# New order of the recurrence's steps, of the first head's projections and of two broadcasts in the mixer layers of a two-block transformer kernel

## The chip, the cores and the metric

One core of one Trainium2 chip runs the whole kernel in one launch. The metric is the device time of one execution in microseconds (us). The engines are TensorE (PE in the profile, with its weight loads as PEld), VectorE (DVE), ScalarE (ACT), GpSimd (POOL) and SyncE (SP, which issues most DMAs). Each takes its own queue of instructions in the order in which the program has put them there, and waits where an instruction needs the result of another engine.

## The reference

The model has two blocks, each of two layers, on one sequence of 512 tokens with 1024 features, all in fp32. The change touches only the mixer of the second block's layers, which the reference writes so:

```python
xn = rms_norm_2(h, attn_norm_g[layer])
u_ssm, u_g, v_g, q, k, v = jnp.split(xn @ w_in[layer], [o1, o2, o3, o4, o5], axis=-1)
y_ssm  = s5_mixer(u_ssm, ...)              # linear recurrence over the tokens, GELU, gated linear unit
y_sgu  = spatial_gating(u_g, v_g, ...)     # tokens mixed in windows of 128
y_diff = diff_attention(q, k, v, ...)      # 4 heads, each softmax(c=0) - lambda * softmax(c=1)
h = h + jnp.concatenate([y_ssm, y_sgu, y_diff], axis=-1) @ w_out[layer]
```

The recurrence takes 256 channels, the gating 256 and the attention 512 (four heads of 128, with two queries and two keys of 64 each). Both y_diff and q and k are normalised row by row.

## The kernel before

A matrix product in fp32 is made of three matmuls in a faster format (mm3, L133 to L135): weights and activations are each split into a high and a low part, on ACT (L95, L97) and on DVE or POOL (L107 to L111). A projection (proj in second_layer) is 24 such matmuls into one bank of PSUM. token_major makes values with tokens on the partitions, in 96 smaller matmuls (L1685 to L1687) for half of the columns.

The code emits instructions for all engines in one stream, and a scheduler with a simulated timeline orders each engine's queue by priority, which is the place in the code; late(n) moves what it encloses back by n places. So the order of the code sets the order of the queues, except where the scheduler sees something ready earlier.

PSUM is divided by tags: `BANKS = dict(mm=2, sc=2, tp=2, o=1, st=1)`. Tag o has one bank. It holds po, the output of a head (L1768), and also, by TG["bk"], the key broadcast that keys makes (L192, from the tile that L187 fills); the table's names for it are pso in both cases. Tag st (psst) holds the output broadcast bo, the rotation's matmuls (L1703) and the row factors of L657. Tag mm (psmm) holds projections and every third group of scores, sc (pssc) other scores and token_major, tp (pstp) the transposed tiles (L279), the statistics (L1713), the gating (L1612, L1613) and the recurrence.

One mixer layer runs so. Two projections make u for the recurrence (L1671). main then makes the gating's values (token_major) and two projections for its other half (L1798), the gating itself (gmlp, L1592 to L1619: L1606 on DVE makes its normalised operand, L1612 and L1613 multiply, L1616 multiplies the result), V in two halves, then the projections, rotation and statistics of head 0 and head 1 (prepare), the key broadcasts (keys) and the attention of four heads (attend), into which the projections of heads 2 and 3 (nx) and, from head 3 on, parts of the output projection (out_part) are woven. s5 is a generator with three steps behind its loads: the matmuls and scans of the recurrence (L1494 to L1513), the matmuls of its output and the write to memory that reorders it (L1523 to L1540), and GELU and gated linear unit (L1543 to L1569). main counts work in `done`, and where it passes an entry of S5_AT the next step of s5 is emitted.

attend walks four tiles of queries: scores (L1750, mask L1751), maximum (L1754, L1756, L1757), exponential (L1760), the difference of the two softmaxes (L1763 to L1765), transposed to pT (L279, L281), product with V into po (L1768). At a head's end ACT reads po twice (L1771, L1772), token_factor makes the row norm (L657 to L664), and L187, L192 and L1782 multiply it in. keys turns the statistics of prepare (L1716 to L1722) into a broadcast (L187, L192) and multiplies the keys (L1732).

The layer runs twice, as mixer 0 from about 1640 to 1905 us and as mixer 1 from about 2262 to 2528 us of the span.

Of the kernel before, what the change touches and what calls it, by code (L numbers as in the profile page):

```python
# [1622 lines left out]
def second_layer(s, L):  # L1623
    nc, a, mixp = s.nc, s.a, s.mixp
# [49 lines left out]
    def token_major(w):  # L1674

        pv = [s.P(TG["tok"]), s.P(TG["tok"])]
        ps = [pv[c // 2][:, (c % 2) * 256:(c % 2) * 256 + 256] for c in range(NT)]
        for g in range(2):
            wh, wl = s.load(w[:, g * 1024:g * 1024 + 1024])
            for k4 in range(4):  # L1680
                k = 4 * g + k4
                for c in range(NT):
                    q = slice(c * 128, c * 128 + 128)
                    w0, w1 = wh[:, k4 * 256:k4 * 256 + 256], wl[:, k4 * 256:k4 * 256 + 256]
                    nc.tensor.matmul(ps[c], s.xh[k][:, q], w0, start=k == 0 and c % 2 == 0, stop=False)  # L1685
                    nc.tensor.matmul(ps[c], s.xh[k][:, q], w1, start=False, stop=False)
                    nc.tensor.matmul(ps[c], s.xl[k][:, q], w0, start=False, stop=k == KT - 1 and c % 2 == 1)  # L1687
        return ps
# [3 lines left out]
    def prepare(h):  # L1692
        sqs, qk = [], []
        for which in range(2):
            ps = proj(4 + 2 * h + which)
            sq, raw, t2 = s.T(), s.T(), s.T()
            t1 = s.A((128, S), F32)
            nc.scalar.activation(raw, ps, AF.Copy)
            nc.scalar.activation(sq, raw, AF.Square)
            nc.vector.scalar_tensor_tensor(t1, raw, gq[:, 2 * which:2 * which + 1], tabs[0], ALU.mult, ALU.mult)  # L1700
            p2 = s.P(TG["perm"])
            with s.late(L_PERM):
                nc.tensor.matmul(p2, perm, raw, start=True, stop=True)  # L1703
            nc.vector.scalar_tensor_tensor(t2, p2, gq[:, 2 * which + 1:2 * which + 2], tabs[1], ALU.mult, ALU.mult)
            nc.gpsimd.tensor_add(t1, t1, t2)
            sqs.append(sq)
            qk.append(t1)
            yield 6
        N = (128, 2, NT, 2)
        ps = s.P(TG["stat"])  # L1710
        for x in range(2):
            for c in range(NT):
                nc.tensor.matmul(ps[:, 8 * x + 2 * c:8 * x + 2 * c + 2], sqs[x][:, c * 128:(c + 1) * 128], s.headind, start=True, stop=True)  # L1713
        v = s.small(N, tag="hfv")
        rb, rb2 = (x.unsqueeze(1).unsqueeze(3).to_broadcast(list(N)) for x in (s.rt, s.rt2))
        nc.vector.tensor_mul(v, ps[:, 0:16].rearrange("p (x c t) -> p x c t", x=2, t=2), rb2)  # L1716

        nc.vector.tensor_scalar(v[:, 0], v[:, 0], 1.0, 64 * EPS, ALU.mult, ALU.add)
        nc.vector.tensor_scalar(v[:, 1], v[:, 1], 1.0 / 64, EPS, ALU.mult, ALU.add)
        y = s.rsqrt(v.rearrange("p x c t -> p (x c t)"), (128, 16))  # L1720
        f = s.small(N, tag="hff", bufs=4)
        nc.vector.tensor_mul(f, y.rearrange("p (x c t) -> p x c t", x=2, t=2), rb)  # L1722
        heads[h] = (f, qk[0], qk[1])
        yield 1

    def keys(h):
        f, Q, Kt = heads[h]
        with s.late(L_KEYS):
            bk = s.bcast_rows(f[:, 1], 2, eng="a", tag=TG["bk"])
        for c in range(2):  # L1730
            r = slice(64 * c, 64 * c + 64)
            nc.vector.tensor_mul(KP[h % 2][c][r], bk[r], Kt[r])  # L1732

    def attend(h):
        f, Q, Kt = heads[h]
        K = KP[h % 2]
        po = s.P("o")
        lsum = s.small((128, 2, NT), tag="dls")
        for i in range(NT):
            n = i + 1  # L1740
            w = n * 128
            q = slice(i * 128, i * 128 + 128)
            m, sc, pp = s.small((128, 2), tag="dm", bufs=6), [], []
            if n <= 2:
                ps = s.P(SCB[(NT * h + i) % len(SCB)])
            for c in range(2):
                if n > 2:
                    ps = s.P(SCB[(NT * h + i) % len(SCB)])
                o = c * w if n <= 2 else 0
                nc.tensor.matmul(ps[:, o:o + w], Q[:, q], K[c][:, :w], start=o == 0, stop=False)  # L1750
                nc.tensor.matmul(ps[:, o + w - 128:o + w], s.identr, s.chunked, start=False, stop=n > 2 or c == 1)  # L1751
                sc.append(ps[:, o:o + w])
                if n > 2:
                    nc.vector.tensor_reduce(m[:, c:c + 1], sc[c], AX.X, ALU.max, negate=True)  # L1754
            if n <= 2:
                nc.vector.tensor_reduce(m, ps[:, :2 * w].rearrange("p (c k) -> p c k", c=2), AX.X, ALU.max, negate=True)  # L1756
            nc.vector.tensor_mul(m, m, f[:, 0, i])  # L1757
            for c in range(2):
                p = s.sp.tile([128, 512], F32, name="p", tag="p")
                nc.scalar.activation(p[:, :w], sc[c], AF.Exp, bias=m[:, c:c + 1], scale=f[:, 0, i, c:c + 1], accum_out=lsum[:, c, i:i + 1])  # L1760
                pp.append(p)
            r = s.small((128, 1), tag="dr", bufs=6)
            nc.vector.reciprocal(r, lsum[:, 1, i:i + 1])  # L1763
            nc.vector.tensor_scalar(r, r, lsum[:, 0, i:i + 1], nlam, ALU.mult, ALU.mult)
            nc.vector.scalar_tensor_tensor(pp[0][:, :w], pp[1][:, :w], r, pp[0][:, :w], ALU.mult, ALU.add)  # L1765
            pT = transposed(s, pp[0], n)
            for j in range(n):
                nc.tensor.matmul(po[:, q], V[j][:, h * 128:h * 128 + 128], pT[:, j * 128:j * 128 + 128], start=j == 0, stop=j == n - 1)  # L1768
            yield 0.6 * n
        ot, sq = s.T(), s.T()  # L1770
        nc.scalar.activation(sq, po, AF.Square)  # L1771
        nc.scalar.activation(ot, po, AF.Copy)  # L1772
        r0 = s.small((128, NT), tag="dr0")
        nc.vector.reciprocal(r0, lsum[:, 0])
        f = token_factor(s, [sq], inds[:, 0], 128, r0, li)
        if h == 3:
            live.append(out_part(s, w_out, *LAST, range(1, KT, 2)))
            for g in live:
                for w in g:
                    pass  # L1780
        bo = s.bcast_rows(f.unsqueeze(2), 1, eng="a")
        nc.vector.tensor_mul(ot, bo, ot)  # L1782
        s.dbg("d_diff%d_%d" % (L, h), ot)
        mix_tile(s, 4 + h, ot, gq[:, 4:5])
        yield 1
# [5 lines left out]
    def main():  # L1791
        ug = []
        vps = token_major(a["w_in_2_vg"][L])
        yield 10
        for x in range(2):
            ps = proj(2 + x)
            t = s.A((128, 512), F32)
            nc.vector.tensor_mul(t, ps, s.rb)  # L1798
            ug.append(t)
            yield 5  # L1800
        yield from gmlp(s, L, gtabs, vps, ug)
        for x in range(2):
            ps = token_major(a["w_in_2_v"][L, x])
            for c in range(NT):
                if x == 0:
                    V[c] = s.A((128, 512), F32)
                nc.scalar.activation(V[c][:, 256 * x:256 * x + 256], ps[c], AF.Copy, scale=s.rt[:, c:c + 1])
            yield 10
        yield from prepare(0)
        keys(0)  # L1810
        yield from prepare(1)
        for h in range(4):
            if h < 3:
                keys(h + 1)
            nx = prepare(h + 2) if h < 2 else iter(())
            if h in PARTS:
                while len(live):
                    next(live[0], None) is None and live.pop(0)
                live.append(out_part(s, w_out, *PARTS[h]))
            for w in attend(h):  # L1820
                x = 0.0
                while live and x < w * PART_RATIO:
                    c = next(live[0], None)
                    if c is None:
                        live.pop(0)
                    else:
                        x += c
                yield w + next(nx, 0)
            for w in nx:
                yield w  # L1830
# [3 lines left out]
    next(side)  # L1834
    done, at, n = 0.0, S5_AT, 0
    for w in main():
        done += w
        while n < len(at) and done >= at[n]:
            next(side, None)
            n += 1  # L1840
# [4 lines left out]
TG = dict(s5b=("tp", "tp"), s5y=("tp", "tp"), perm="st", gm="tp", bk="o", stat="tp", tok="sc")  # L1845
L_PERM = 0
L_KEYS = 40
S5_AT = [12, 34, 60]
SCB = ["sc", "sc", "mm"]
PARTS = {3: (0, 4)}  # L1850
LAST = (4, 6)
# [310 lines left out]
```

## Time and profile before

| | us |
|---|---|
| timed runs, median of 3 (lowest to highest) | 2903.78 (2902.26 to 2911.31) |
| profiled execution | 2889.64 |
| its span | 2887.9 |
| TensorE busy in it | 2756.0 |
| mean granted clock of TensorE | 0.972 of full speed |

The span runs from the first to the last instruction; the profiled execution's own time has 1.7 us more around it. The profile gives each engine's busy time, what ended its idle time (the releaser), and the TensorE clock that was granted, as a share of full speed. Times in the rows are microseconds from the start of the span.

### The profile page before, as it was taken

What the parts mean: (1) busy time and instruction counts of PE and PEld (TensorE: products, weight loads), DVE (VectorE), ACT (ScalarE), POOL (GpSimd) and SP (SyncE); (2) the same over time, 40 slices, a digit from 0 to 9 for tenths busy, and PEclk for the clock granted to TensorE, in tenths of its full rate; (3) what the DMA queues carried; (4) which work ended last, traced back from release to release, by engine and by line L of the source; (5) the groups of instructions that cost most, each with busy time, mean ns of one, the idle gap of its engine ahead of it and who ended that gap; (6) DMA issues with size and microseconds to landing.
All of it is one profiled execution on the core that took longest, in us unless ns stands there. A gap on an engine that the chain in (4) does not pass through costs nothing.

```text
span 2887.9 us, 41501 instructions
## 1 busy us (share of the span) xinstructions
PE 2756.0 (95%) x15403; PEld 2344.7 (81%) x15403; DVE 1745.4 (60%) x3366; ACT 1271.7 (44%) x2305; POOL 820.8 (28%) x668
## 2 busy tenths in 40 slices
PE   7989999999999899999999789999999898999999
PEld 6766678888888799999999777778888776788887
DVE  3667669465454567666666536776375536775473
ACT  3555553223322466666666414444243224443342
POOL 3310024232112154555555221032023211122120
PEclk8979999999999899999999899999999999999999
DMA  3200123334332276776777732132333320232322
GB/s 129 94 27 22 34 79 131 95 130 140 105 95 66 75 249 203 247 225 225 242 225 249 217 109 67 34 109 87 106 97 103 124 70 15 76 95 89 108 89 94
DMA packets 123192, 344.67 MB, mean 119 GB/s; under 512 B 16610, under 2 KB 28162, under 8 KB 122468
## 3 DMA queue, kind: packets, MB, share of 16 engines
q1 hardware_dynamic: 111968, 320.60, 35.3%
q0 software_dynamic: 5680, 17.19, 1.8%
q10 hardware_dynamic: 5332, 4.14, 0.5%
q8 instruction: 123, 2.02, 0.3%
q14 instruction: 89, 0.73, 0.1%
HBM read 326.39 MB, written 15.48 MB: 118 GB/s over the span
## 4 chain that ended last, share of the span: by engine, by line
PE 55%; DVE 4%; POOL 3%; ACT 2%; issue 2%; DMA 1%; SPq 0%; another core or an unknown queue 0%; POOLq 0%; DVEq 0%; ACTq 0%
PE psmm L1050 5%; PE psmm L133 5%; PE psmm L134 5%; PE psmm L135 5%; PE pssc L1050 5%; PE pstp L133 3%; PE pstp L135 3%; PE pstp L134 3%; PE pssc L133 3%; PE pssc L135 3%; PE pssc L134 3%; PE psmm L1051 2%; PE pssc L1051 2%; POOL wlo L109 1%; DVE wlo L111 1%
## 5 line engine op out<-in xcount | busy, mean ns | idle before, releaser
L95 ACT ACTIVATE whi<-raw 128x1024 fp32r<-128x1024 f32 (+5 forms) x687 | 629.1, 918 | 900.7 <-PE psmm L134 326.9
L111 DVE TENSOR_TENSOR wlo<-raw,whi 128x1024 fp32r<-128x1024 f32 (+4 forms) x605 | 728.8, 1208 | 381.1 <-ACT whi L95 345.5
L1050 PE MATMUL psmm<-A,whi 128*128 128x320 f32 x1120 | 302.9, 348 | 3.4 <-DVE T L1056 1.8
L133 PE MATMUL psmm<-xh,whi 128*128 128x512 f32 x688 | 277.7, 405 | 11.6 <-ACT xh L97 8.3
L134 PE MATMUL psmm<-xl,whi 128*128 128x512 f32 x688 | 274.2, 399 | 3.9 <-DVE xl L107 3.9
L1050 PE MATMUL pssc<-A,whi 128*128 128x320 f32 x992 | 272.7, 351 | 2.3 <-ACT whi L95 1.4
L135 PE MATMUL psmm<-xh,wlo 128*128 128x512 f32 x688 | 273.8, 398 | 0.1
L1051 PE MATMUL psmm<-A,wlo 128*128 128x160 f32 x1120 | 265.5, 239 | 0.0
L1051 PE MATMUL pssc<-A,wlo 128*128 128x160 f32 x992 | 238.6, 242 | 5.2 <-DVE wlo L111 4.8
L109 POOL TENSOR_TENSOR wlo<-raw,whi 128x1024 fp32r<-128x1024 f32 (+2 forms) x82 | 196.3, 2397 | 163.6 <-ACT whi L95 138.6
L109 POOL TENSOR_TENSOR A<-T,A 128x160 fp32r<-128x160 f32 (+2 forms) x166 | 184.0, 1110 | 123.7 <-ACT A L95 123.5
L1050 PEld LDWEIGHTS psmm<-A,whi 128*128 128x128 f32 x1120 | 210.2, 188 | 7.0 <-DVE T L1056 5.3
L1051 PEld LDWEIGHTS psmm<-A,wlo 128*128 128x128 f32 x1120 | 213.6, 191 | 0.6
L1051 PEld LDWEIGHTS pssc<-A,wlo 128*128 128x128 f32 x992 | 191.1, 193 | 9.4 <-DVE wlo L111 7.2
L1050 PEld LDWEIGHTS pssc<-A,whi 128*128 128x128 f32 x992 | 187.7, 190 | 4.5 <-ACT whi L95 2.7
L1876 POOL TENSOR_TENSOR T<-T 128x512 f32<-128x512 f32 x44 | 57.1, 1297 | 415.8 <-DVE T L1873 358.7
L135 PE MATMUL pssc<-xh,wlo 128*128 128x512 f32 x448 | 175.2, 391 | 0.0
L134 PE MATMUL pssc<-xl,whi 128*128 128x512 f32 x448 | 175.2, 391 | 0.0
L133 PE MATMUL pssc<-xh,whi 128*128 128x512 f32 x448 | 174.9, 390 | 0.0
L95 ACT ACTIVATE A<-T 128x160 fp32r<-128x160 f32 (+2 forms) x178 | 85.8, 482 | 185.2 <-POOL T L1072 97.4
L133 PEld LDWEIGHTS psmm<-xh,whi 128*128 128x128 f32 x688 | 132.2, 193 | 41.0 <-ACT xh L97 8.3
L134 PEld LDWEIGHTS psmm<-xl,whi 128*128 128x128 f32 x688 | 132.1, 192 | 35.0 <-DVE xl L107 6.8
(614 smaller groups left out, 6137.3 us busy)
## 6 DMA issues: line engine op xcount, KB each, us to landing
raw<-moe_gu SPq DMA_DIRECT2D x176, 512.0 KB, 4.5
raw<-w_up_t SPq DMA_DIRECT2D x88, 512.0 KB, 3.5
raw<-moe_dn SPq DMA_DIRECT2D x64, 384.0 KB, 3.5
raw<-ffn_gu SPq DMA_DIRECT2D x44, 512.0 KB, 3.7
raw<-moe_dn SPq DMA_DIRECT2D x64, 320.0 KB, 3.3
raw<-od_w_in_t SPq DMA_DIRECT2D x24, 512.0 KB, 3.5
raw<-w_in_t SPq DMA_DIRECT2D x24, 512.0 KB, 3.5
raw<-w_down_t SPq DMA_DIRECT2D x32, 384.0 KB, 3.0
```

The source lines that it names most:

```text
L95: nc.scalar.activation(out, x, AF.Copy)
L109: nc.gpsimd.tensor_sub(out, x, h.bitcast(F32))
L111: nc.vector.tensor_sub(out, x, h.bitcast(F32))
L133: nc.tensor.matmul(ps, wh, xh, start=first, stop=False)
L134: nc.tensor.matmul(ps, wh, xl, start=False, stop=False)
L135: nc.tensor.matmul(ps, wl, xh, start=False, stop=last)
L1050: nc.tensor.matmul(ps[:, :2 * CAP], wh, x, start=first, stop=False)
L1051: nc.tensor.matmul(ps[:, :CAP], wl, x[:, :CAP], start=False, stop=last)
L1876: nc.gpsimd.tensor_mul(acc[1], acc[1], acc[0])
```

## The change

It adds and removes no instruction; it moves some. S5_AT goes from [12, 34, 60] to [26, 48, 72], so that the three steps of the recurrence are emitted later: the first behind the gating, the second behind prepare(0), the third behind prepare(1). prepare(0) is emitted ahead of the second half of V. keys(h+1) is emitted behind the first tile of attend(h) and no more ahead of attend(h). The output broadcast bo of the first three heads is put back by L_OUT = 40 places. The new code's lines behind L1781 are one to three higher.

```diff
--- before.py
+++ after.py
@@ -1778,7 +1778,8 @@
             for g in live:
                 for w in g:
                     pass
-        bo = s.bcast_rows(f.unsqueeze(2), 1, eng="a")
+        with s.late(L_OUT if h < 3 else 0):
+            bo = s.bcast_rows(f.unsqueeze(2), 1, eng="a")
         nc.vector.tensor_mul(ot, bo, ot)
         s.dbg("d_diff%d_%d" % (L, h), ot)
         mix_tile(s, 4 + h, ot, gq[:, 4:5])
@@ -1800,24 +1801,25 @@
             yield 5
         yield from gmlp(s, L, gtabs, vps, ug)
         for x in range(2):
+            if x == 1:
+                yield from prepare(0)
             ps = token_major(a["w_in_2_v"][L, x])
             for c in range(NT):
                 if x == 0:
                     V[c] = s.A((128, 512), F32)
                 nc.scalar.activation(V[c][:, 256 * x:256 * x + 256], ps[c], AF.Copy, scale=s.rt[:, c:c + 1])
             yield 10
-        yield from prepare(0)
         keys(0)
         yield from prepare(1)
         for h in range(4):
-            if h < 3:
-                keys(h + 1)
             nx = prepare(h + 2) if h < 2 else iter(())
             if h in PARTS:
                 while len(live):
                     next(live[0], None) is None and live.pop(0)
                 live.append(out_part(s, w_out, *PARTS[h]))
-            for w in attend(h):
+            for i, w in enumerate(attend(h)):
+                if i == 1 and h < 3:
+                    keys(h + 1)
                 x = 0.0
                 while live and x < w * PART_RATIO:
                     c = next(live[0], None)
@@ -1845,7 +1847,8 @@
 TG = dict(s5b=("tp", "tp"), s5y=("tp", "tp"), perm="st", gm="tp", bk="o", stat="tp", tok="sc")
 L_PERM = 0
 L_KEYS = 40
-S5_AT = [12, 34, 60]
+S5_AT = [26, 48, 72]
+L_OUT = 40
 SCB = ["sc", "sc", "mm"]
 PARTS = {3: (0, 4)}
 LAST = (4, 6)
```

The queue of DVE around the gating of mixer 0, before. psmm is a projection, pssc the gating's values, pstp a product of the recurrence or of the gating.

```order
L1798 TENSOR_TENSOR A_19180<-psmm_19155,rb_18896 128x512 [waits PE_49]
...
L111 TENSOR_TENSOR wlo_19529<-raw_19526,whi_19528 128x1024 [waits DMAHW6_49,PE_49,Activation_49]
L1502 TENSOR_TENSOR A_19219<-pstp_19182,s5E_19008 128x512 [waits DMAHW4_49,PE_49]
...
L1511 TENSOR_TENSOR A_19231<-A_19219,s5E_19008 128x512 [waits DVE_49]
L1507 SCALAR_TENSOR_TENSOR A_19224<-A_19216,A_19224 128x512 [waits Pool_49]
L1511 TENSOR_TENSOR A_19236<-A_19224,s5E_19008 128x512 [waits DVE_49]
L1798 TENSOR_TENSOR A_19272<-psmm_19247,rb_18896 128x512
L1606 SCALAR_TENSOR_TENSOR A_19297<-pssc_19039,rsy4_19283,vgain_18900 128x256
...
L1616 TENSOR_TENSOR A_19180<-pstp_19305,A_19180 64x512 [waits PE_49]
```

The same place of DVE now:

```order
L1799 TENSOR_TENSOR A_19180<-psmm_19155,rb_18896 128x512 [waits PE_49]
...
L1799 TENSOR_TENSOR A_19213<-psmm_19188,rb_18896 128x512 [waits PE_49]
L1606 SCALAR_TENSOR_TENSOR A_19238<-pssc_19039,rsy4_19224,vgain_18900 128x256 [waits DVE_49]
...
L111 TENSOR_TENSOR wlo_19462<-raw_19459,whi_19461 128x1024 [waits DMAHW6_49,Activation_49]
L1616 TENSOR_TENSOR A_19180<-pstp_19246,A_19180 64x512 [waits PE_49]
...
L111 TENSOR_TENSOR wlo_19504<-raw_19501,whi_19503 128x1024 [waits DMAHW7_49,Activation_49]
L1502 TENSOR_TENSOR A_19319<-pstp_19282,s5E_19008 128x512 [waits DMAHW4_49,PE_49]
...
L1511 TENSOR_TENSOR A_19331<-A_19319,s5E_19008 128x512 [waits DVE_49]
...
L1511 TENSOR_TENSOR A_19336<-A_19324,s5E_19008 128x512 [waits DVE_49]
```

The four L1606 and the L1616 now stand ahead of the recurrence's L1502 to L1511, and not behind them.

The queue of TensorE at the end of head 0 of mixer 0, before. pso_19920 is po of head 0, pso_20178 the key broadcast of head 2, psst_20140 the row factor and psst_20166 the output broadcast of head 0; A_18927 is the keys of head 2.

```order
L1768 MATMUL pso_19920<-pT_20128,A_19457 128x128
L133 MATMUL psmm_20279<-xh_18727,whi_20275 128x512 [waits PE_49,Activation_49]
...
L657 MATMUL psst_20140<-pack_all_81,T_20135 128x2 [waits Activation_49]
...
L1750 MATMUL pssc_20375<-A_18930,A_19833 128x512 [waits PE_49,Activation_49]
...
L192 MATMUL psst_20166<-pack_all_81,T_20164 128x128 [waits Activation_49]
...
L192 MATMUL pso_20178<-pack_all_81,T_20176 128x128 [waits Activation_49]
...
L1750 MATMUL psmm_20453<-A_18927,A_19977 128x128 [waits DVE_49]
```

The same place now; here pso_19911 is po of head 0, pso_20001 the key broadcast of head 1, A_18929 and A_18930 are the keys of head 1, and psmm_20279 is a projection of head 3.

```order
L1768 MATMUL pso_19911<-pT_20128,A_19457 128x128
L657 MATMUL psst_20140<-pack_all_81,T_20135 128x2 [waits Activation_49]
...
L192 MATMUL pso_20001<-pack_all_81,T_19999 128x128 [waits PE_49,Activation_49]
...
L1750 MATMUL pssc_20179<-A_18929,A_19793 128x128 [waits DVE_49]
...
L1750 MATMUL pssc_20179<-A_18930,A_19793 128x128 [waits DVE_49]
...
L192 MATMUL psst_20166<-pack_all_81,T_20164 128x128 [waits PE_49,Activation_49]
...
L133 MATMUL psmm_20279<-xh_18727,whi_20275 128x512 [waits Activation_49]
```

Before, the broadcast in bank o behind head 0 was that of head 2, and scores of head 1 stood ahead of it; now it is that of head 1, and all scores of head 1 stand behind it.

## Rows read from the trace of the kernel before

**Rows 1.** The page: busy time of each engine, and engines on the chain that ended last.
```profile
PE 2756.0 (95%) x15403; PEld 2344.7 (81%) x15403; DVE 1745.4 (60%) x3366; ACT 1271.7 (44%) x2305; POOL 820.8 (28%) x668
...
PE 55%; DVE 4%; POOL 3%; ACT 2%; issue 2%; DMA 1%; SPq 0%; another core or an unknown queue 0%; POOLq 0%; DVEq 0%; ACTq 0%
```

**Rows 2.** TensorE's waits, mixer 0 (1630 to 1910 us): total us, times, longest.
```profile
PE pstp L1612 <- DVE A L1606: 8.7, 1, 8.7
...
PE pso L192 <- ACT T L187: 3.9, 1, 3.9
PE psmm L133 <- ACT p L1760: 3.7, 2, 2.0
PE psst L192 <- ACT T L187: 2.9, 1, 2.9
...
PE pso L1768 <- ACT pT L281: 0.7, 1, 0.7
```

**Rows 3.** TensorE's waits, mixer 1 (2255 to 2530 us), lines that differ.
```profile
PE psmm L133 <- ACT p L1760: 3.9, 2, 2.2
PE pso L192 <- ACT T L187: 3.8, 1, 3.8
...
PE pssc L1750 <- ACT p L1760: 0.8, 1, 0.8
```

**Rows 4.** Windows: span of each, busy us (instructions) by engine, granted clock, DMA.
```profile
1680.80:1691.00 10.20, 4.79 (x21) 4.49 (x22) 6.37 (x9) 0.00 (x0) 6.05 (x5) 0.50 0.01 2
1694.30:1697.80 3.50, 3.50 (x17) 3.41 (x17) 0.68 (x1) 0.00 (x0) 0.00 (x0) 0.52 0.00 0
1700.00:1720.00 20.00, 20.00 (x193) 18.63 (x193) 3.82 (x4) 4.66 (x8) 1.15 (x3) 1.00 0.16 54
1730.00:1735.00 5.00, 5.00 (x24) 4.14 (x23) 1.89 (x2) 1.56 (x3) 0.00 (x0) 1.00 1.05 379
1759.30:1766.10 6.80, 4.22 (x10) 2.89 (x11) 5.07 (x14) 2.86 (x5) 0.53 (x1) 0.50 0.00 1
1813.90:1817.30 3.40, 3.10 (x10) 2.21 (x11) 2.91 (x5) 3.07 (x7) 0.00 (x0) 0.50 0.00 0
1830.60:1838.00 7.40, 5.39 (x27) 4.40 (x27) 5.22 (x22) 4.57 (x12) 0.00 (x0) 1.00 0.00 1
1840.00:1860.00 20.00, 20.00 (x113) 16.58 (x112) 15.16 (x47) 11.77 (x29) 0.00 (x0) 1.00 0.09 27
2452.20:2459.00 6.80, 4.90 (x12) 3.85 (x13) 3.68 (x21) 3.75 (x11) 0.00 (x0) 0.50 0.00 0
```

**Rows 5.** Timeline around the gating, mixer 0: start, us, instruction, [idle before <-releaser].
```profile
1675.29 1.06 ACT L95 ACTIVATE whi<-raw 128x1024 fp32r<-128x1024 f32 x1 [4.38 <-PE psmm L134]
...
1675.41 2.09 PE L1494 MATMUL pstp<-s5U,A 128*64 128x64 f32 x64
...
1684.38 0.69 DVE L1511 TENSOR_TENSOR A<-A,s5E 128x512 f32<-128x512 f32 x1
...
1685.59 1.65 DVE L1606 SCALAR_TENSOR_TENSOR A<-pssc,rsy,vgain 128x256 f32<-128x256 f32 x4
...
1687.38 2.50 POOL L1513 TENSOR_TENSOR A<-A 128x512 f32<-128x512 f32 x2
```

**Rows 6.** Timeline between head 0's statistics and the first key broadcast, mixer 0.
```profile
1758.36 0.23 DVE L1716 TENSOR_TENSOR hfv<-pstp,rt 128x16 f32<-128x16 f32 x1
...
1761.20 0.63 ACT L187 ACTIVATE T<-hff 128x512 f32<-128x512 f32 x1 [4.32 <-DVE hff L1722]
```

**Rows 7.** Timeline of ACT and of DVE in the attention of mixer 0.
```profile
1816.60 1.40 DVE L1732 TENSOR_TENSOR A<-pso,A 64x512 f32<-64x512 f32 x2
...
1826.81 0.59 ACT L281 ACTIVATE pT<-pstp 128x512 f32<-128x512 f32 x1
...
1828.64 0.60 ACT L1771 ACTIVATE T<-pso 128x512 f32<-128x512 f32 x1 [0.53 <-PE pso L1768]
...
1830.14 0.67 ACT L1760 ACTIVATE p<-pssc,dm,hff 128x384 f32<-128x384 f32 x1 [0.41 <-DVE dm L1757]
```

## Prediction

> **What bounds the kernel now.** I read the page first. TensorE is busy for 95% of the span and carries 55% of the chain that ended last [rows 1], so a change in order can only give back what TensorE waits, and what it loses at the lower clock after a wait. The two mixer layers, the only stages touched, were then read by the table of TensorE's waits, each layer in its own stretch. Mixer 0 has five waits that the change can reach: 8.7 us at the gating matmuls (L1612) for DVE, 3.9 us at the first key broadcast (L192 into bank o), 3.7 us in two pieces for a bank that the exponentials read, 2.9 us at the first output broadcast (L192 into bank st), 0.7 us for a transposed tile [rows 2]. Mixer 1 repeats them, with 3.8 for 3.9, 3.9 for 3.7 and 0.8 for 0.7; its other lines read as in mixer 0 [rows 3]. Last I read windows around the waits for the granted clock. Behind the gating wait TensorE works 4.79 us and then 3.50 us at about half clock (1.2 of 2.4 GHz), behind the key broadcast 4.22 us, behind the output broadcast 3.10 us, and in mixer 1 another 4.90 us behind the bank wait of 2.2 us; behind mixer 0's bank wait of 2.0 us there is none [rows 2 to 4]. Work at half clock costs half of its time: 2.4 + 1.75, 2.1, 1.55 and 2.45 us.
>
> **Why the gating waits.** The gating needs L1606, which needs only the vector projection that was long done. But it stands on DVE behind the recurrence: DVE takes the multiplications and scans that the L1494 matmuls release from 1677.5, ends them with L1511 at 1685.07, and reaches L1606 at 1685.59 [rows 5]. TensorE has nothing else queued ahead of L1612.
>
> **Part 1, the recurrence's steps come later.** The order of DVE now has L1606 ahead of the recurrence, and TensorE meets two projection matmuls, then L1612, then token-major V, and only then L1494. What is late next is the weight of those two matmuls: ACT makes it (L95) from 1675.29 to 1676.35, while TensorE has run dry shortly before 1675.5 [rows 5]; I count 0.9 us. The gain per layer is 8.7 - 0.9 = 7.8, plus 4.15 of clock: 11.95 us.
> The three moved steps need cover of their own. From the end of L1494 (1677.50) to the end of L1513 (1689.88) the recurrence takes 12.4 us [rows 5]. Between L1494 and L1530 the new order has 46 token-major matmuls (193 matmuls of this size and smaller in 20 us, so some 4.8 us), 46 projection matmuls (24 take about 5 us, so 9.6) and the 32 of L1523 (3.3): 17.7 us, over 5 us to spare [rows 4]. The last step (the GELU on ACT, DVE and POOL, then L1562) gets prepare(1)'s projections and most of one of prepare(2)'s as cover; with the durations of the trace I estimate 3 to 4 us of slack. Its ten DMAs on POOL's queue move with it and are queued ahead of POOL's additions for the projections as before; the loads on SP change place with a neighbour only. Cost taken: nothing; if that cover were gone, each us of lateness is one us of waiting.
>
> **Part 2, the first head's projections before the second half of V.** Today the statistics of head 0 are followed at once by the key broadcast: L1716 starts at 1758.36, L187 at 1761.20, so 2.84 us of small DVE steps and 0.63 us on ACT stand in front of L192 [rows 6], with nothing to do on TensorE. In the new order 76 token-major and 24 projection matmuls stand between, 7.9 + 5 = 13 us [rows 4]. The wait goes, 3.9 + 2.1 of clock = 6.0 us. Parts 1 and 2 together give 17.9 us a layer, **35.8 us** in two.
>
> **Part 3, keys(h+1) behind the first tile of attend(h), and part 4, the output broadcast later.** Here lies the price. The key broadcast writes the bank of tag o, which has one buffer, and the head's output po has the same bank. Before, bk(h+1) was written ahead of po(h), under the previous work. Now it follows po(h): it must wait until L1771 and L1772 have read po, and then L1732 must make the keys before any score of the next head. As TensorE takes its queue in order, I walked that queue from head to head and put the durations of the trace behind each wait.
> At a head's end the queue reads L279, L1768, L657, L192 (keys), six score groups, L192 (output). L1768 waits for L281, 0.59 and some 0.2 us from one engine to the next: 0.8. L657 waits for L1771, 0.60: 0.8. The scores wait for L192 and for L1732, 1.40 for both halves, behind three small steps of the output factor: 1.3. The output's L192 waits for the rest of that factor (small steps on DVE, like the 2.84 us of rows 6) and for L187: 0.8. That is 3.7 us at each of the first two boundaries [rows 7]. At the third I count 3.2, since output-projection matmuls cover a part.
> In head 0, L1703 (the second half of head 2's rotation) waits for a copy that now stands on ACT behind L187 of keys(1), which waits for the statistics: 2.8 + 0.6 + 0.6 less 1.0 of other matmuls is 3.0 us [rows 6]; the bank wait of 1.7 us behind it stays. In head 1 I count four waits of 0.4 to 1.6, 3.9 us in all, in head 2 two of 3.1 and 1.5, where L279 waits for an L1765 queued on DVE behind reductions, and L1768 for an L281 behind exponentials. The sum is 3.7 x 2 + 3.2 + 4.7 + 3.9 + 4.6 = 23.8 us a layer, 47.6 in two. It is a hand count along in-order queues; a wait that is paid early shortens the later ones, so its lower bound is what the attention waits today.
> What it replaces: 3.7 + 2.9 + 0.7 + 1.55 of clock = 8.85 us in mixer 0, and 3.9 + 2.9 + 0.8 + 1.55 + 2.45 = 11.6 in mixer 1 [rows 2 to 4], together **20.45 us**.
> The clock: waits of 2.9 and 3.9 us were followed by half clock, one of 2.2 was and one of 2.0 was not [rows 2 to 4], so the small waits may cost nothing in clock or up to about 2 us each. With five places a layer (three boundaries and the waits of 3 us) the bounds are 0 and 20 us for both layers; I take two places a layer, **8 us**, since two of the five single waits are of the length that was always followed by a dip.
> Of this, the Trainium skill ("TensorE: Matmul & The Clock Gate", section "A second HAM failure mode: psum-queue depth-cycling") says that frequent short idling of TensorE between groups of matmuls, from cycling through PSUM banks, makes the clock swing between its two levels. The trace here agrees only in part, with one dip behind 2.2 us and none behind 2.0 us. By that rule the upper bound of 20 us would hold and the sum below would be 11.4 us instead of -0.6.
>
> **The sum.** -35.8 - 20.45 + 47.6 + 8 = -0.6 us. Against the profiled execution's 2889.64 us that is 2889.0. That execution lies 14 us under the median of the timed runs, 2903.78, so I put the difference on the median: 2903.1, the forecast. A measurement of this kernel can tell about 0.3%, 8.7 us, from no change.
>
> **The rivals.**
> Faster: the heads' waits overlap, so that half of the count holds, 23.8 + 4 of clock. The sum is then -35.8 - 20.45 + 27.8 = -28.4: 2875 us. For it speaks that in 1840 to 1860 us TensorE today is busy throughout, with the same steps waiting behind one another [rows 4]; against it that there the keys were ready a head ahead. Were the attention to wait just as today, it would be -35.8: 2868.
> Slower, by the chain through bank o: at a boundary everything of the next head hangs on po being read (1.3), L192 and L1732 (0.7 + 1.4) [rows 7], the scores (0.7), and the maximum, the exponential (0.67) and the steps L1763 to L1765 (an estimate of 2.5 together), about 6.6 us with nothing that another head could lend, of which I have counted 3.7 or 3.2 as uncovered. If half of the rest (some 9 us a layer) is uncovered too, it adds 9 us: 2912; if all of it, 18 us: 2921. It decides the sign from 4.7 us more a layer. For it speaks that after head 1 there is no projection of a later head left.
> Slower, by the clock: the lower clock behind each of the five places a layer, 2915 us.
> Not doing what it says: the gating still waits on DVE because DVE's multiplication ahead of it (L1799 in the new code) or the weight comes late; with half of part 1's gain gone, 12 us, it is 2915.
>
> **How the numbers follow.** No change beyond 0.3%: 0.40. Faster: 0.33. Slower: 0.27 (chain through bank o 0.14, clock 0.08, gating 0.05). The likeliest case by itself spans 2895 to 2912. The range that is to hold the time 8 times in 10 reaches further to both sides: down to 2872, below the faster rival's 2875 and above the 2868 of an attention that waits just as today, and up to 2919, above the three slower cases but for the wholly uncovered chain. I put one in ten on each side outside.
>
> **What would show it.** In the new profile: no wait at L1612 beyond about 1 us, and full clock in the 20 us behind it (part 1); no wait at the first L192 into pso (part 2); new lines in the table of TensorE's waits for L192 pso, L657, L1750 <- DVE A L1732 and L1703 <- ACT, summing to some 24 us a layer (parts 3 and 4). If that sum is under 14, the faster rival holds; if it is over 29, or if the granted clock falls below 0.9 at most boundaries, a slower one does. A wait at L1530 or L1562 would mean that the moved steps lack their cover.

## The result, and the profile after

The changed kernel takes 2921.93 us (median of 5 runs) against 2903.78: the ratio of the runs is 1.0059, with an interval of 1.0037 to 1.0081. It is slower by 0.6%, some 17 us; no change was forecast, and the upper end of the range was 2919. Executions of one kernel differ in the clock by chance (42 of the kernel before, timed with the experiments, took 2890 to 2910 us at mean granted clocks of 0.973 to 0.965), but the five of the changed kernel all lie at 0.963 to 0.965. In the two profiled executions the span grows by 25.6 us, from 2887.9 to 2913.5, and the page shows this:

```profile
span 2913.5 us, 41487 instructions
...
PE 2784.4 (96%) x15403; PEld 2357.2 (81%) x15403; DVE 1757.5 (60%) x3366; ACT 1273.7 (44%) x2305; POOL 822.7 (28%) x668
...
PE 55%; POOL 3%; DVE 3%; ACT 2%; issue 2%; DMA 0%; SPq 0%; ACTq 0%; another core or an unknown queue 0%; POOLq 0%; DVEq 0%
```

TensorE does the same 15403 matmuls, but is busy for 28.4 us more than in [rows 1]. It does not wait more (its idle time in the whole span is 131.9 us before and 129.1 after); it takes longer for the same work. The mixers as whole stretches say where: from the first L1671 of a mixer to a fixed matmul behind it (number 10800 and number 13800 of TensorE's queue), in windows with busy us by engine, instructions and granted clock. First before:

```profile
1659.00:1893.40 234.40, 210.65 (x1224) 171.77 (x1223) 139.08 (x341) 87.71 (x186) 43.96 (x44) 0.95 0.25 74
2276.90:2522.70 245.80, 221.08 (x1277) 180.63 (x1276) 143.84 (x343) 91.85 (x191) 47.62 (x46) 0.94 0.21 64
```

and after:

```profile
1663.20:1911.00 247.80, 225.76 (x1231) 178.99 (x1230) 144.67 (x341) 89.40 (x186) 44.26 (x44) 0.91 0.24 69
2294.50:2548.30 253.80, 231.51 (x1276) 184.39 (x1276) 150.22 (x343) 92.84 (x191) 48.82 (x46) 0.92 0.20 62
```

Mixer 0 is longer by 13.4 us and mixer 1 by 8.0, 21.4 together. The other 4.2 us of the span stand before mixer 0 (it starts at 1663.2 and not at 1659.0), where nothing was moved. That is within chance: in the twelve profiles of this case the work ahead of mixer 0 is the same, yet it lasts 1658.3 to 1669.3 us, and TensorE works 75 to 98 us of it at half clock (82.0 before, 89.0 after). One from near each end, the kernel before and the run of parts 1 and 2 (below):

```profile
0.00:1659.00 1659.00, 1580.09 (x9578) 1375.02 (x9579) 1025.85 (x2173) 813.32 (x1571) 576.58 (x475) 0.97 0.45 144
0.00:1669.10 1669.10, 1588.84 (x9584) 1381.10 (x9585) 1022.08 (x2174) 813.79 (x1571) 575.87 (x475) 0.96 0.45 143
```

In the mixers TensorE's idle time, length less busy time, is 23.75 + 24.72 = 48.5 us before and 22.04 + 22.29 = 44.3 after: 4.2 us less. The clock is lower in both.

TensorE's waits in mixer 0 after (total us, times, longest), where [rows 2] stood:

```profile
PE pstp L279 <- DVE p L1765: 2.5, 3, 2.0
PE pso L1768 <- ACT pT L281: 2.5, 4, 1.0
PE psst L657 <- ACT T L1771: 2.2, 3, 0.7
PE psst L1703 <- ACT T L1698: 2.1, 1, 2.1
PE psmm L133 <- ACT p L1760: 1.9, 2, 1.7
PE pssc L1750 <- ACT p L1760: 1.7, 3, 0.9
PE pssc L1750 <- DVE A L1732: 1.7, 2, 0.8
...
PE psmm L1750 <- DVE A L1732: 1.2, 1, 1.2
PE pstp L279 <- DVE rst L169: 1.1, 1, 1.1
PE psmm L133 <- ACT whi L95: 0.9, 1, 0.9
```

The lines of L1612 and of both L192 are gone (the 0.9 us at L133 is the gating's wait for the weight). In their place stand many waits of 0.7 to 2.1 us, on just the instructions that the walk along the queue had named: L657 for L1771, the scores for L1732, L1703 for its copy, L1768 for L281. The windows around them, and the 20 us behind the gating's start, show the clock:

```profile
1680.00:1700.00 20.00, 19.08 (x168) 13.73 (x167) 8.42 (x13) 2.12 (x2) 0.00 (x0) 1.00 0.10 33
1775.30:1785.60 10.30, 7.64 (x15) 4.82 (x16) 4.75 (x12) 4.61 (x11) 1.26 (x1) 0.50 0.00 0
1795.80:1802.60 6.80, 5.96 (x21) 4.68 (x20) 4.42 (x17) 1.74 (x3) 0.00 (x0) 0.50 0.01 2
1819.70:1833.40 13.70, 10.76 (x36) 8.16 (x36) 5.23 (x25) 2.83 (x5) 0.00 (x0) 0.50 0.00 1
1840.20:1847.00 6.80, 5.65 (x17) 4.17 (x16) 3.56 (x12) 3.32 (x9) 0.00 (x0) 0.50 0.00 1
1860.70:1864.10 3.40, 3.40 (x12) 2.61 (x11) 1.77 (x11) 0.45 (x2) 0.00 (x0) 0.50 0.00 0
2406.80:2413.60 6.80, 5.26 (x13) 2.94 (x11) 3.41 (x13) 2.13 (x4) 0.34 (x1) 0.50 0.00 0
2427.30:2434.10 6.80, 5.95 (x23) 4.77 (x22) 3.77 (x16) 1.42 (x4) 0.00 (x0) 0.50 0.00 0
2451.20:2464.80 13.60, 10.42 (x37) 7.89 (x36) 6.18 (x29) 2.83 (x5) 0.00 (x0) 0.50 0.00 0
2471.60:2481.90 10.30, 8.98 (x23) 6.55 (x24) 4.06 (x13) 3.44 (x11) 0.00 (x0) 0.50 0.00 0
```

The gating runs at full clock now. In the attention TensorE works 33.4 us at half clock in mixer 0 and 30.6 in mixer 1 (the busy time of PE, the number behind each row's length, summed). Half of that, 32.0 us, is lost; before it was 1.55 in mixer 0 and 1.55 + 2.45 in mixer 1 [rows 4].

The account of the 21.4 us: idle time -4.2; work at half clock, all of the mixers, from 35.9 to 70.8 us of busy time, so a loss of 35.4 and no more of 17.95, +17.4; and 8 us that are neither. Taken by line and put at full clock, 7.2 of these 8 us stand on four lines that now wait: 3.4 on L1750, 1.5 each on L279 and L1768, 0.8 on L657. The ends of matmuls are modelled in a trace, so part of a wait may show there as busy time; that is argued only.

### The profile page after: what moved, and what is told of

Its sections match the earlier page's. It is cut to its first block, busy times and chain, and to the rows that moved or that the text cites. A ratio compares the mean times of both kernels' runs of the same rounds, so it can differ in the third digit from the quotient of the medians.

```text
span 2913.5 us, 41487 instructions
## 1 busy us (share of the span) xinstructions
PE 2784.4 (96%) x15403; PEld 2357.2 (81%) x15403; DVE 1757.5 (60%) x3366; ACT 1273.7 (44%) x2305; POOL 822.7 (28%) x668
## 4 chain that ended last, share of the span: by engine, by line
PE 55%; POOL 3%; DVE 3%; ACT 2%; issue 2%; DMA 0%; SPq 0%; ACTq 0%; another core or an unknown queue 0%; POOLq 0%; DVEq 0%
PE psmm L1050 5%; PE psmm L133 5%; PE psmm L134 5%; PE psmm L135 5%; PE pssc L1050 4%; PE pstp L133 3%; PE pstp L134 3%; PE pstp L135 3%; PE pssc L133 3%; PE pssc L134 3%; PE pssc L135 3%; PE psmm L1051 2%; PE pssc L1051 2%; POOL wlo L109 1%; ACT whi L95 1%
## 5 line engine op out<-in xcount | busy, mean ns | idle before, releaser
L133 PE MATMUL psmm<-xh,whi 128*128 128x512 f32 x688 | 276.5, 403 | 13.5 <-ACT xh L97 8.3
L133 PE MATMUL pssc<-xh,whi 128*128 128x512 f32 x448 | 174.7, 390 | 0.0
L133 PEld LDWEIGHTS psmm<-xh,whi 128*128 128x128 f32 x688 | 132.8, 193 | 43.0 <-ACT xh L97 8.3
```

The lines of the kernel that those rows point to most:

```text
L133: nc.tensor.matmul(ps, wh, xh, start=first, stop=False)
```

## The experiments

All ratios are to the kernel before, timed on the same chip in the same job. The changed kernel and the runs come from different jobs, so they are compared with each other by these ratios. Each run has one profile, of one execution.

### Parts 1 and 2 alone

```diff
         for x in range(2):
+            if x == 1:
+                yield from prepare(0)
...
-        yield from prepare(0)
...
-S5_AT = [12, 34, 60]
+S5_AT = [26, 48, 72]
```

> The kernel before with parts 1 and 2 alone: the recurrence's steps later, the first head's projections ahead of the second half of V; the keys stay ahead of attend. Theory A (parts 1 and 2 gain what the waits at L1612 and at the first L192 cost, and the whole loss comes from the keys behind the first tile): 35.8 us less than before, near 2868, ratio 0.988; in its profile no wait over 1 us at L1612 and none at the first L192 into pso, TensorE at half clock only in the attention, about as long as before. Theory B (the work moved out of the waits makes the attention wait longer by itself, whatever the keys do): within 9 us of the kernel before.

Measured: 0.9935 (0.9911 to 0.9958), 2880.06 us, 19 us less. The direction of theory A, and half of its size. The mixers' windows:

```profile
1669.10:1897.80 228.70, 215.05 (x1219) 173.70 (x1218) 142.29 (x341) 87.83 (x185) 45.63 (x44) 0.94 0.27 74
2281.20:2515.00 233.80, 219.51 (x1277) 178.09 (x1276) 147.43 (x343) 92.30 (x192) 49.18 (x46) 0.96 0.22 67
```

TensorE's idle time in the mixers falls from 48.5 to 27.9 us, 20.5 less, near the 23.4 of waiting expected. But the clock gave nothing back in sum: the work at half clock goes from 35.9 to 39.2 us. These are the stretches at half clock in the attention, the last two of them in mixer 1:

```profile
1778.70:1785.60 6.90, 5.42 (x16) 3.79 (x17) 5.35 (x12) 2.86 (x5) 1.64 (x1) 0.51 0.00 0
1812.90:1823.10 10.20, 9.82 (x33) 7.63 (x34) 5.83 (x9) 4.21 (x8) 1.70 (x1) 0.50 0.00 0
1833.30:1840.20 6.90, 5.84 (x16) 4.57 (x16) 3.42 (x16) 3.59 (x8) 0.00 (x0) 0.51 0.00 1
2393.10:2400.00 6.90, 5.11 (x14) 3.48 (x15) 5.28 (x13) 2.86 (x5) 1.36 (x1) 0.51 0.00 0
2427.30:2437.50 10.20, 9.66 (x32) 7.47 (x33) 5.97 (x10) 4.21 (x8) 1.70 (x1) 0.50 0.01 2
```

The wait of 2.9 us at the output broadcast is the same as in [rows 2], and so is the order of the queue around it; the half clock behind it lasts 10.2 us and not 3.4 [rows 4]. The first and fourth rows stand behind a new wait, 2.8 us at the key broadcast of head 1.

### Part 3 alone

```diff
-            if h < 3:
-                keys(h + 1)
...
-            for w in attend(h):
+            for i, w in enumerate(attend(h)):
+                if i == 1 and h < 3:
+                    keys(h + 1)
```

> The kernel before with part 3 alone: keys(h+1) behind the first tile of attend(h). Theory A: the mixers of the changed kernel were 21 us slower in the profile though parts 1 and 2 gained about 36, so this part costs some 57 us: near 2960, ratio 1.020, with over 30 us more of TensorE's work at half clock in the attention than before. Theory B: half of that or less, under 2930, since the attention's waits of the changed kernel would come from parts 1 and 2.

Measured: 1.0175 (1.0143 to 1.0206), 2946.68 us, 50 us more: theory A, a little under its 57 us. The mixers' windows in this run (as above):

```profile
1658.60:1918.80 260.20, 228.22 (x1224) 182.91 (x1224) 142.75 (x341) 88.17 (x186) 43.11 (x44) 0.88 0.23 66
2302.30:2572.40 270.10, 238.17 (x1278) 191.05 (x1277) 148.27 (x343) 92.61 (x191) 47.49 (x46) 0.89 0.19 58
```

They are longer than before by 50.1 us: 15.4 of idle time (from 48.5 to 63.9), 30.6 of clock (the loss goes from 17.95 to 48.5, the busy time at half clock from 35.9 to 97.0), 4.1 not placed. So in this profile the keys behind the first tile cost twice as much by the clock as by the waits. Ahead of mixer 0 it has 81.4 us at half clock, as much as before (82.0), and its four executions lie at 0.958 to 0.960, so chance does not make this.

### The same order of the code, another bank for the keys

```diff
-TG = dict(..., bk="o", ...)
+TG = dict(..., bk="tp", ...)
```

> The changed kernel with the key broadcast in a bank of tag tp (two buffers, shared with transposed tiles) and not in po's bank; the order of the code is that of the changed kernel. If the shared bank o is what makes the next head's keys wait for the end of a head: near the run of parts 1 and 2 alone, 2868 to 2880, with the waits L1750 <- A L1732 and L657 <- T L1771 gone. If the place in the code is what makes the keys late: it stays near the changed kernel, 2915 or more.

Measured: 0.9960 (0.9940 to 0.9980), 2886.99 us. With two banks at hand the queue has the keys of head 1 behind the second tile of head 0 and no more behind its last, and the waits L657 <- T L1771 and L1750 <- A L1732 are gone. Against the changed kernel that is 1% less, so the shared bank of tag o, and not the place in the code by itself, makes the keys late. The median is a little above the 2868 to 2880 expected; two other waits are new there, in mixer 0 1.6 us of the keys' L192 for L187 and 1.4 us of L1703 for L1783.

### Part 1 alone, part 2 alone

```diff
-S5_AT = [12, 34, 60]
+S5_AT = [26, 48, 72]
```

> The kernel before with part 1 alone, S5_AT of [26, 48, 72]. By the waits: 7.8 us of waiting and 4.15 us of clock a layer less, 23.9 us in two: near 2880, ratio 0.992, the wait of 3.9 us at the first key broadcast still there. If the recurrence's later steps have no cover without the moved projections: a new wait at L1530 or L1562 takes some of that back, and the time is over 2890.

Measured: 0.9929 (0.9902 to 0.9955), 2877.23 us. As much as parts 1 and 2 together. Its waits in mixer 0:

```profile
PE psst L192 <- ACT T L187: 2.9, 1, 2.9
PE pso L192 <- ACT T L187: 2.8, 1, 2.8
...
PE pstp L1612 <- DVE A L1606: 1.2, 1, 1.2
```

The pso line is not the wait that was expected to stay: it stands at 1771 us, at the key broadcast of head 1, while that of head 0 has 29 matmuls of head 1's projections between its statistics and itself and waits no more. The queue says why. The statistics of head 0 (L1713) need a bank of tag tp, and both were held by L1562; with the recurrence's third step later, the statistics come first, and those of head 1 come late instead. Before, the third step is emitted where `done` reaches 60, between the projections and the statistics of head 0; with 72 it is emitted at 73, between the projections and the statistics of head 1, and not behind the whole of prepare(1), as the section on the change has it.

```diff
         for x in range(2):
+            if x == 1:
+                yield from prepare(0)
...
-        yield from prepare(0)
```

> The kernel before with part 2 alone: prepare(0) ahead of the second half of V. Theory: the wait of 3.9 us at the first key broadcast comes from the statistics (L1713), which wait for the banks of tag tp that L1562 of the gated linear unit holds; with prepare(0) emitted earlier the statistics come ahead of it. Then the wait is gone in this run (3.9 + 2.1 of clock a layer): 12 us less, ratio 0.996; the gating's 8.7 us stay. If the wait is only exchanged for one of the next head's statistics behind L1562: a new wait of 2 to 4 us at the second L192 into pso, and within 5 us of the kernel before.

Measured: 0.9928 (0.9901 to 0.9955), 2878.03 us, more than expected. The wait at the key broadcast is gone, and so is most of the gating's, since 24 matmuls of head 0's projection now stand ahead of L1612:

```profile
PE pstp L1612 <- DVE A L1606: 3.1, 1, 3.1
```

The third step, at 60, now comes behind the whole of prepare(0), so neither head's statistics wait for its banks. So parts 1 and 2 are two ways to the same gain, and they were added in the prediction as if each had its own.

### The gated linear unit's products in another bank

```diff
     for m in range(2):
-        ps = s.P("tp")
+        ps = s.P("sc")
```

> The kernel before with one change: the two products of the gated linear unit (L1562) in banks of tag sc and not tp. If the statistics waited for those banks: L1713 of head 0 stands 38 projection matmuls ahead of the first key broadcast, the waits at the first L192 into pso are gone without any change of order, and the time is some 12 us less, ratio 0.996. If the first key broadcast is late for another reason: no difference.

Measured: 0.9992 (0.9977 to 1.0008), 2896.32 us: no difference. The place of the wait is right, the price is not. The wait at the first key broadcast is gone without any move in the code, so it did come from L1562's banks. But the idle time falls by 4.8 us only (48.5 to 43.7), since L133 now waits 4.9 us in three pieces for banks that the exponentials read, against 3.7 [rows 2], and the work at half clock rises by 3.5 us.

### The recurrence's third step later still

```diff
-S5_AT = [26, 48, 72]
+S5_AT = [26, 48, 90]
```

(part 1 alone, with this)

> Part 1 alone, but with the third step of the recurrence at 90 and not 72, so that the statistics of head 1 also come ahead of L1562. Against the run of part 1 alone, where TensorE waited 2.8 us at the second L192 into pso: that wait is gone, 5.6 us and its clock of some 5 us a layer less; 0.988 to 0.990 of the kernel before. If L1562 finds no cover there (the attention): a new wait at L1562, and about the time of part 1 alone, 0.993.

Measured: 0.9910 (0.9882 to 0.9938), 2870.43 us, just short of the 0.988 to 0.990 expected. The wait at the second key broadcast is gone as expected, and L1562 does not wait. What it gains over part 1 alone lies within the uncertainty of the two runs; L133 <- p L1760 grows to 5.7 us in mixer 0 and L192 into psst to 3.2.

### Matmuls that nobody reads

```diff
+        if h < 3:
+            d = s.P("tp")
+            for k in range(3):      # behind the last L1768 of the head
+                with after(s, last):
+                    last = nc.tensor.matmul(d[:, 128 * k:128 * k + 128], V[0][:, 0:128], pT[:, 0:128], start=True, stop=True)
+            d = s.P("tp")
+            last = s.last_bk        # behind L192 of the next head's keys
+            for k in range(4):
+                ...
```

> The changed kernel with 7 added matmuls of 128x128 at the end of each of the first three heads, whose results nobody reads: 3 between the last L1768 and L657 (which waits some 0.7 us for L1771 there), 4 behind the key broadcast's L192 (where the scores wait 0.8 to 1.2 us for L1732). At 0.22 us each they are as long as the waits that they fill, 42 in all. If the lower clock behind the many small waits is what costs: TensorE's work at half clock falls from 33 us in mixer 0's attention and 31 in mixer 1's to 20 or less, and the time is 10 to 15 us under the changed kernel, near 1.001 of the kernel before. If the waits themselves cost and the clock does not depend on them: the waits are only filled, and the time stays within 4 us of the changed kernel, 1.005 to 1.007, or goes up.

Measured: 1.0024 (1.0009 to 1.0039), 2904.6 us: with 42 matmuls more than the changed kernel it is 0.35% faster, about 10 us; by the two intervals it is 2 to 18. TensorE's queue at the end of head 0, L1780 being the added matmuls (each of the four is recorded twice) and L1751 what L1750 was:

```profile
1791.81 0.92 PE L657 MATMUL psst<-pack_all,T 128*128 128x2 f32 x7
1792.59 0.64 PE L192 MATMUL pso<-pack_all,T 128*128 128x128 f32 x4
1793.06 1.06 PE L1780 MATMUL pstp<-pT,A 128*128 128x128 f32 x8
1794.07 0.49 PE L1751 MATMUL pssc<-A 128*128 128x128 f32 x2
...
1798.13 0.91 PE L1751 MATMUL pssc<-A 128*128 128x384 f32 x2 [1.34 <-DVE dm L1755]
```

No wait for L1771 or L1732 is left, though a new one of 1.3 us for a maximum stands behind them, and this boundary, which lay in a stretch of half clock in the changed kernel (1795.8 to 1802.6), runs at full clock. The stretches at half clock that remain:

```profile
1772.00:1782.20 10.20, 7.36 (x14) 4.63 (x15) 4.63 (x12) 4.79 (x11) 1.26 (x1) 0.50 0.00 0
1816.40:1823.20 6.80, 6.80 (x34) 6.80 (x33) 2.55 (x10) 1.09 (x2) 0.00 (x0) 0.50 0.01 4
1830.00:1840.30 10.30, 8.13 (x21) 5.78 (x22) 4.82 (x15) 4.19 (x13) 0.00 (x0) 0.50 0.00 1
2400.00:2410.30 10.30, 7.93 (x16) 5.00 (x17) 4.75 (x12) 4.32 (x11) 1.26 (x1) 0.50 0.00 0
2444.40:2451.20 6.80, 6.80 (x35) 6.71 (x33) 2.86 (x11) 1.08 (x2) 0.00 (x0) 0.50 0.00 0
2458.10:2468.30 10.20, 8.30 (x21) 5.93 (x22) 4.56 (x15) 4.14 (x12) 0.00 (x0) 0.50 0.01 2
```

They hold 45.3 us of work against 64.0, which is worth 9.3 us, as much as the gain. TensorE's waits from the first to the last head fall by 3.8 and 4.2 us, about as much time as the added matmuls take, so what is left over is the clock's price. The fall to 22.3 and 23.0 us is a little short of the 20 expected.

### Two versions beyond

```diff
-S5_AT = [12, 34, 60]
+S5_AT = [26, 48, 90]
...
-        bo = s.bcast_rows(f.unsqueeze(2), 1, eng="a")
+        def finish():
+            bo = s.bcast_rows(f.unsqueeze(2), 1, eng="a")
...
-            for w in attend(h):
+            for i, w in enumerate(attend(h)):
+                if i == 1 and late:
+                    late.pop(0)()
```

> The run with the recurrence's third step at 90, and the output broadcast of each of the first three heads emitted behind the second tile of the next head (the code's place, not a priority). There L192 into psst waited 3.2 us for L187 in mixer 0. With scores and products of the next head ahead of it that wait goes: if the clock behind it (9.8 us at half clock in mixer 0, 3.3 in mixer 1) goes with it, 5 to 12 us less than that run, 0.987 to 0.990 of the kernel before; if the waits only move to the exponentials (L133 or L1750 <- p L1760), about the same, 0.991.

Measured: 0.9882 (0.9861 to 0.9904), 2860.98 us, faster than both kernels; against the run that it varies, 0.9910, the gain is within the two intervals. The wait of L192 into psst is gone; in the mixers 25.2 us of idle time and 22.9 us of work at half clock are left, against 48.5 and 35.9 before. One wait has grown:

```profile
PE psmm L133 <- ACT p L1760: 6.6, 2, 3.4
```

```diff
-S5_AT = [12, 34, 60]
+S5_AT = [26, 48, 90]
...
-TG = dict(..., bk="o", ...)
+TG = dict(..., bk="tp", ...)
```

> The run with the recurrence's third step at 90, and the key broadcast in a bank of tag tp and not in po's. With the keys emitted ahead of attend, bank o was never late for them: if it holds nothing up, within 3 us of that run, 0.991; if po of the next head did wait for the keys to be read, 3 to 8 us less; if the transposed tiles wait for the two banks of tp, 3 to 10 us more.

Measured: 0.9932 (0.9914 to 0.9950), 2873.98 us. Its interval overlaps that of the run that it varies, 0.9910; the output broadcast waits 6.9 us in two pieces there. With the keys emitted ahead of attend, the bank of tag o holds nothing up that is worth a move.

## Why the prediction was wrong

**The step that failed** is the clock. In the mixers the sum counted 9.3 us more of waiting (47.6 new less the 38.3 that go) and 10 us less lost at half clock (8 new less 12.5 and 5.55). The profiles have 4.2 us less of waiting, 17.4 us more lost at half clock, and the 8 us on the waiting lines. So the waits came out 13.5 us better than counted, and the clock some 27 us worse.

**The waits that go.** Right in place and kind. The gating's wait went from 8.7 to the 0.9 us for the weight that was counted, at full clock behind it; the wait of the first key broadcast went; L1530 and L1562 never waited. Wrong in one thing: parts 1 and 2 were priced one after the other, 23.9 + 12 us, while each alone gains some 20 us and both gain 19. What failed here is "the wait goes, 3.9 + 2.1 of clock" under part 2: the trace had the statistics' wait for a bank that L1564 reads directly ahead of them, and moving the recurrence alone settles it. And "cost taken: nothing" under part 1 overlooked that the third step then holds those banks ahead of head 1's statistics: with the keys ahead of attend this is a new wait of 2.8 us a layer.

**The clock given back.** The sum took 12.5 us off for half clock that would vanish with the two waits. It vanished there, but for 3.4 us of work in mixer 0, and came back in the attention: in the run of parts 1 and 2 the loss of the mixers is 19.6 us against 17.95. Together that is 35.8 expected and 17.7 found in the profiles, 19 in the timed runs.

**The attention's waits.** Most stand where the walk along the queue put them, and are shorter; the 0.8 us counted for the output's L192 at each boundary do not appear. Counted were 23.8 us a layer; the waits over 0.25 us from the first to the last head add up to 17.1 in mixer 0 and 17.5 in mixer 1. Over the run of parts 1 and 2 the changed kernel has 16.4 us more of idle time, where the count had some 33 over the attention of before. The two waits of 3.0 and 3.1 us came out at 2.1 and 2.0, which the walk did not foresee.

**The clock of the new waits.** 8 us were taken, with 20 as upper bound, for both layers; the loss in the attention was 32.0. Of this, 17.9 stand in the run of parts 1 and 2 already, with no new wait but the 2.8 us, and the keys behind the first tile add the rest. The bound came from single waits of 2 to 4 us, each followed by 3.1 to 4.9 us of work at half clock [rows 4]. That small waits in a row bring stretches of up to 13.7 us with 10.8 us of work no row of before could show. The rival "slower, by the clock" is what happened, beyond its price of 2915 us and together with the smaller gain of parts 1 and 2; it had 0.08. Of the rule that spoke for it, the Trainium skill ("TensorE: Matmul & The Clock Gate", section "A second HAM failure mode: psum-queue depth-cycling": frequent short idling between groups of matmuls, from cycling through PSUM banks, makes the clock swing), the runs now agree as far as short waits go: no wait of the changed kernel's attention is over 2.1 us, and 64.0 us of its work ran at half clock.

**The shared bank.** Right: the run with the keys in tag tp takes the loss back without any move in the code.

**Part 4.** It does nothing: with L_OUT = 0 the queues of TensorE, DVE and ACT come out the same row by row; the runs have L_OUT at 0 or at 40. It was priced together with part 3, at nothing of its own, but not named as idle.

**The sum by measured terms.** Parts 1 and 2 -17.7 us, the keys behind the first tile on top of them +39.1 (16.4 of idle time, 15.8 of clock, 6.9 that are neither): +21.4 in the mixers, +25.6 in the span with the 4.2 us ahead of them, and 17 us in the timed runs. The profiled execution of the kernel before lies 14 us under its median, that of the changed kernel 7 under, which is 7 of the 8.6 us between the last two numbers.

## What to carry to other kernels

Where a change trades one long wait of TensorE for several short ones, price the clock of the stretch, not only the waits: in this kernel the short ones cost as much again by the half clock that followed them, and twice as much in one run. Two moves that each free the same blocked resource gain once; look at what the waiting instruction's bank is held by before adding them. And a one-buffer bank shared by the end of one step and the start of the next makes them serial as soon as the code emits the second one's claim behind the first.

## What the hardware showed that was not expected

The same wait, 2.9 us in the same place of the same queue, was followed by 3.1 us of work at half clock in one kernel [rows 4] and by 9.8 us in another (1812.9 to 1823.1), whose queue is the same there and differs only ahead of it. The two mixers of one run differ in the same way; in the run with the third step at 90 the stretches behind the output broadcast of mixers 0 and 1, where the waits are 3.2 and 2.9 us, are

```profile
1800.60:1810.90 10.30, 9.83 (x33) 7.64 (x34) 5.90 (x10) 4.31 (x8) 1.70 (x1) 0.50 0.00 0
...
2415.00:2418.40 3.40, 3.28 (x10) 2.39 (x11) 2.90 (x6) 3.07 (x7) 0.00 (x0) 0.50 0.02 5
```

So what a single wait costs in clock is not a property of the wait, and a sum of such costs from one trace is uncertain by several us for each. Part of it is chance: the unchanged work ahead of mixer 0 had 75 to 98 us at half clock in the twelve profiles. How much is chance and how much is the work ahead of the wait stays open, since no kernel was profiled twice.

And work that nobody reads made a kernel faster: 42 matmuls, some 9 us of TensorE's time by an estimate of 0.22 us each, brought about 10 us.
